# A float32 hybrid encoder layer: both heads' near-score products ahead of both minima, the second norm's reciprocal straight from PSUM, and three differences behind a split

## The chip, the cores and the metric

One core of a Trainium2 chip runs the whole layer as one program. The metric is the device time of one execution in microseconds (us). The layer has one batch element, 1024 positions, a model width of 1024 and float32 inputs and outputs. A difference of about 0.2% (2.6 us) is what the measurement of this kernel can tell from none.

## The reference, cut to what matters

```python
u = rms_norm(h, mix_norm_gain);  proj = u @ w_in
aq, ak, av, dqkv, dgate, da, db = split(proj)
# A: band attention, 8 heads of 64, chunks of 64, own chunk + 8 past ones
scores = einsum(q, k_band) * 64**-0.5 + rel_bias ;  p = softmax(where(valid, scores, min)) ; o = p @ v_band
# B: gated DeltaNet, 4 heads of 128: conv + SiLU, L2 norms, chunked delta rule over a state S, gated norm
h = h + concat[rms_norm(A), B] @ w_out
z = rms_norm(h, ffn_norm_gain) @ w_ff1          # norm over the width, per position: x * rsqrt(mean(x*x) + EPS)
h = h + square(relu(z)) @ w_ff2
```

## The kernel before, in words

**Stages.** The program first projects the input (0 to about 355 us of the profiled execution), then runs attention and the delta rule interleaved (to about 597 us), then the output projection `out_proj` (to about 684 us), the first feed-forward product `ff1` (to about 990 us) and the second, `ff2`. A float32 operand of the large products is split into a high and a low part (`split`, line 201: a cast on ScalarE, line 202, and a difference on VectorE or GpSimd, line 203), and three TensorE matmuls stand for one.

**Who sets the order.** Tile's scheduler orders each engine's instructions, with one exception: inside `attention` the TensorE order is the order in which the code is written (`manual_schedule`). A planner in that function, with a `Clock` of assumed costs, picks at each step the next piece: `score`, `flip`, `multiply`, `finish`, `turn`, or a step of the delta rule (`delta_state` S, `delta_out` O, `delta_merge` M, `delta_fin` F). Each engine runs its queue in order.

**A unit of attention** is one group of four heads g, one tile of 128 queries t, and one pair of heads pp: 2 x 8 x 2 = 32 units. `score` makes, for each of the two heads e of the pair, the near scores (the last 256 keys) into one half of one PSUM tile `t_sb` (`product`, matmuls at line 914) and takes their minimum with the bias (VectorE, line 930; a second small instruction reads the accumulated minimum into `t_nm`). Then come the far scores `t_sa` of each head in a PSUM tile of its own, with a minimum at line 941 that starts from the near one. ScalarE takes the exponentials (lines 949 and 953). `flip` transposes them (`t_tpb` at line 970, `t_tpa` at 986) and copies the results out on VectorE or ScalarE (lines 976, 991), `multiply` makes the product with the values (`t_o`, 1009), and `finish` transposes and scales it (1031, 1033); for the second group, eight times in all, `finish` also makes a root mean square on ScalarE and GpSimd (`t_r`) and scales by it on VectorE (line 1040). Tile puts semaphores between instructions of two engines that touch the same PSUM tile in the same bank, whichever columns they touch.

**The second norm** is in `ff1`. `norm_col` (line 1277) sums the squares into eight columns `hcol` with one matmul each (line 1283), multiplies and adds EPS on VectorE (line 1285), and takes the reciprocal (line 1287) into `r_col`. `norm_row` spreads `r_col` over all partitions (`hrow`, line 1293), and ScalarE copies that to `r2` (line 1295). The result is the square of the norm's scale, since the hidden values are squared.

**The second feed-forward product** uses a scheme of seven products instead of eight for each block kb of four (`p1`, `p5`, `p2`, `p3`, `p6`, `p7`, `p4`). Each `product` calls a `prep` that makes sums and differences of quarters on VectorE, then splits both operands (the low parts are named `p50a_l`, `p50b_l` for product 5 of block 0), then multiplies (line 1425). The differences the change touches are those of line 1508 (`s1 - a11`, for product 3) and line 1517 (`a11 - a21`, for product 7), each once per half i, so four per block.

Of the kernel before, what the change touches and what calls it, by code (L numbers as in the profile page):

```python
# [8 lines left out]
F32 = mybir.dt.float32  # L9
F32R = mybir.dt.float32r  # L10
AF = mybir.ActivationFunctionType
ALU = mybir.AluOpType
AX = mybir.AxisListType

P = 128
SEQ = 1024
DM = 1024
NKT = DM // P
NT = SEQ // P
# [9 lines left out]
EPS = 1e-6  # L29
# [12 lines left out]
LATENCY, MARGIN = 250, 400  # L42
# [5 lines left out]
class Clock:  # L48
# [16 lines left out]
    def pe(self, cost):  # L65
        self.now += cost
        return self.now + LATENCY
# [32 lines left out]
def hymba_kernel(  # L100
# [63 lines left out]
    warm = bank(ps_o, "warm")  # L164
    for i in range(WARM):
        nc.tensor.matmul(warm[:, 0:P], ones, ones, start=True, stop=True)
    ident = cpool.tile([P, P], F32, name="ident")
    make_identity(nc, ident)
    tri_u = mpool.tile([P, P], F32, name="tri_u")
# [658 lines left out]
    def attention(after, delta, values, outputs):  # L828
# [89 lines left out]
        def score(g, t, pp):  # L918
            T = tiles[g, t]
            n, k0, kb, nm = (T[k] for k in ("n", "k0", "kb", "nm"))  # L920
            wa, wb = (kb - k0) * P, (t + 1 - kb) * P
            cost = 0
            done = T["done"][pp] = []
            bk = bank(ps_a, f"{n}_sb{pp}")
            sb = page("u" if g or t > 1 else "wr", f"{n}_pb{pp}")
            for e in range(2):
                i = 2 * pp + e
                c = slice(e * 256 + 256 - wb, e * 256 + 256)
                cost += product(g, T, i, bk, c.start, kb, t + 1)
                nc.vector.tensor_tensor_reduce(sb[:, c], bk[:, c], new[g][pp][:, c], -1.0, 3.0e38,  # L930
                                               ALU.add, ALU.min, nm[:, 4 + i:5 + i])
                done.append(on("v", 180 + wb * 1.25, pe(30 + wb * 0.9)))
            give("a", done[1])
            sa = [None, None]
            if wa:
                for e in range(2):
                    i = 2 * pp + e
                    bk = bank(ps_a, f"{n}_sa{i}")
                    cost += product(g, T, i, bk, 0, k0, kb)
                    sa[e] = page("u", f"{n}_pa{i}")  # L940
                    nc.vector.tensor_tensor_reduce(sa[e][:, 0:wa], bk[:, 0:wa], old[g][i][:, 384 - wa:384], -1.0,  # L941
                                                   nm[:, 4 + i:5 + i], ALU.add, ALU.min, nm[:, i:i + 1])
                    done[e] = on("v", 305 + wa * 1.04, pe(max(234, wa * 0.92)))
                    give("a", done[e])
            for e in range(2):
                i = 2 * pp + e
                c = slice(e * 256 + 256 - wb, e * 256 + 256)
                m = nm[:, i:i + 1] if wa else nm[:, 4 + i:5 + i]
                nc.scalar.activation(sb[:, c], sb[:, c], AF.Exp, bias=m, scale=-1.0,  # L949
                                     accum_out=T["sums"][:, 4 + i:5 + i])  # L950
                done[e] = on("s", 480 + wb * 0.85, done[e])
                if wa:
                    nc.scalar.activation(sa[e][:, 0:wa], sa[e][:, 0:wa], AF.Exp, bias=m, scale=-1.0,  # L953
                                         accum_out=T["sums"][:, i:i + 1])
                    done[e] = on("s", 480 + wa * 0.83, done[e])
            T["s"][pp] = sa, sb
# [282 lines left out]
    def ff1(R, started, psw, pools):  # L1239
# [37 lines left out]
        def norm_col():  # L1277

            acc = page2("ut4", "acc")
            nc.sync.dma_start(out=acc, in_=sq_dr)  # L1280
            ps = psw.tile([P, 1024], F32, tag="bk", name="hcol")
            for q in range(NT):
                nc.tensor.matmul(ps[:, q:q + 1], acc[:, q * P:(q + 1) * P], ones[:, 0:1], start=True, stop=True)
            with tc.issue_after(held[-1][2]):
                m = nc.vector.tensor_scalar(r_col, ps[:, 0:NT], 1.0 / DM, EPS, ALU.mult, ALU.add)
                with tc.issue_after(m.ins), tc.high_priority():
                    nc.vector.reciprocal(r_col, r_col)

        def norm_row():

            ps = psw.tile([P, 1024], F32, tag="bk", name="hrow")
            for q in range(NT):
                nc.tensor.matmul(ps[:, q * P:(q + 1) * P], r_col[:, q:q + 1].broadcast_to([P, P]), ident,
                                 start=True, stop=True)
            nc.scalar.copy(r2.rearrange("p a t -> p (a t)"), ps)

        def block(sb):
            def lw(tag, name, kh, c):
# [102 lines left out]
    def ff2(psw, pools):  # L1401
# [7 lines left out]

        y = {i: [wide(t, 0), wide(t, 1)] for i, t in y.items()}  # L1410
        y[7] = [page2("y7", f"y7_{i}") for i in range(2)]
        side = [0]

        def load_h(t, j, hf, m):
            nc.sync.dma_start(out=two(t), in_=h_dr[j, hf, :, 2 * m:2 * m + 2, :])
# [1 line left out]
        def product(name, prep, by_rows=False):  # L1417
            t = "AB"[side[0]]
            side[0] ^= 1
            ps = [psw.tile([P, 1024], F32, tag="bk", name=f"{name}{m}") for m in range(4 if by_rows else 2)]  # L1420
            def step(i, k, q):
                (ah, al), (bh, bl) = ops[i]
                s = slice(k * 512 + q * P, k * 512 + (q + 1) * P)
                for m, (l, r) in enumerate(((ah, bh), (ah, bl), (al, bh))):
                    nc.tensor.matmul(part(ps[q], 0) if by_rows else part(ps[q // 2], q % 2), l[:, s], part(r, k),  # L1425
                                     start=(i + k + m == 0), stop=(i + k + m == 4))

            ops = []
            for i in range(2):
                ab = []  # L1430
                for o, src in zip("ab", prep(i)):
                    hi = page2("h" + t, f"{name}{o}{i}_h", F32R)
                    lo = page2("l" + t, f"{name}{o}{i}_l", F32R)
                    split(src, hi, lo, nc.scalar, nc.vector)
                    ab.append((hi, lo))
                ops.append(ab)
                if not by_rows:
                    for k in range(2):
                        for q in range(4):
                            step(i, k, q)  # L1440
            if by_rows:
                for q in range(4):
                    for i in range(2):
                        for k in range(2):
                            step(i, k, q)
            return ps
# [7 lines left out]
        for kb in range(nb):  # L1454
# [50 lines left out]
                return s1[i], b11[i]  # L1505

            def prep3(i):
                tt(s1[i], s1[i], a11[i], ALU.subtract)
                tt(a12[i], a12[i], s1[i], ALU.subtract)
                return a12[i], b22[i]  # L1510

# [2 lines left out]
                return s1[i], b11[i]  # L1514

            def prep7(i):
                tt(a21[i], a11[i], a21[i], ALU.subtract)
                tt(b12[i], b22[i], b12[i], ALU.subtract)
                return a21[i], b12[i]

# [3 lines left out]

            accumulate(1, product(f"p1{kb}", lambda i: (a11[i], b11[i])))
            accumulate(5, product(f"p5{kb}", prep5))
            accumulate(2, product(f"p2{kb}", lambda i: (a12[i], b21[i])))
            if last:
                merge(nc.gpsimd, 2, 1)
# [124 lines left out]
```

## Time and profile before

| what | value |
| --- | --- |
| time, median of 3 runs | 1321.31 us (1320.35 to 1322.62) |
| the profiled execution's own time | 1308.9 us |
| its span, first to last instruction | 1307.1 us |
| TensorE busy / weight loads busy | 1249.8 us (96%) / 1038.5 us (79%) |
| VectorE, ScalarE, GpSimd busy | 933.2, 548.1, 289.9 us |
| mean granted TensorE clock | 0.993 |

The profiled execution is 12.4 us shorter than the median of the timed runs; 1.8 us of its time lie outside the span. The profile's names: PE is TensorE's matmul, PEld its weight load, DVE VectorE, ACT ScalarE, POOL GpSimd. `L914` is line 914 of the kernel before; `t_sb<-ks,t_q` is output and inputs by the program's names. A row of waits gives the total, the number and the longest of the waits of one engine at one line for one releaser.

### The profile page before, as it was taken

The page shows a single profiled execution, that of the slowest core. Times are in us where ns is not written, and L with a number is a line of the kernel's source. Part 1 is how long each engine was busy: PE and PEld are TensorE (multiplying, and loading weights), DVE is VectorE, ACT ScalarE, POOL GpSimd, SP SyncE. Part 2 cuts the span into 40 slices and gives each one's busy share as a digit, 9 for nine tenths or more (in the row PEclk, how much of TensorE's full clock was granted, in tenths as well). Part 3 has the DMA queues.
Part 4 walks back from the last instruction along what each step waited for, and adds up shares of the span by engine and source line. Part 5 has one row for each costly group of instructions (what it writes and reads, how often), then busy time and mean ns, then how long its engine had stood idle before and what let it go on. Part 6 is the DMA issues. An engine that isn't in the chain of part 4 may idle for free.

```text
span 1307.1 us, 18026 instructions
## 1 busy us (share of the span) xinstructions
PE 1249.8 (96%) x6684; PEld 1038.5 (79%) x6684; DVE 933.2 (71%) x1389; ACT 548.1 (42%) x899; POOL 289.9 (22%) x486
## 2 busy tenths in 40 slices
PE   9999999999988888789999999999999999999998
PEld 7778878788777777677778788888887888888886
DVE  7899978655045556664528877766668988897988
ACT  8232222232254545562527444444464443333331
POOL 5425451444023333364220000000000000000034
PEclk9999999999999999899999999999999999999999
DMA  6214354566574423113423343233257733423002
GB/s 220 70 44 142 94 150 127 101 177 161 182 220 112 128 73 88 33 58 115 143 88 130 129 140 102 94 100 126 99 193 272 261 112 98 144 66 111 17 33 96
DMA packets 135400, 158.53 MB, mean 121 GB/s; under 512 B 31761, under 2 KB 79377, under 8 KB 134801
## 3 DMA queue, kind: packets, MB, share of 16 engines
q1 hardware_dynamic: 117216, 135.11, 33.7%
q10 hardware_dynamic: 18096, 22.29, 5.0%
q8 instruction: 52, 0.85, 0.3%
q14 instruction: 36, 0.29, 0.1%
HBM read 109.91 MB, written 47.45 MB: 120 GB/s over the span
## 4 chain that ended last, share of the span: by engine, by line
PE 57%; DVE 8%; ACT 2%; issue 2%; POOL 2%; DMA 1%; POOLq 1%; SPq 0%; DVEq 0%; ACTq 0%
PE q L1329 21%; PE p L1425 20%; PE op L221 5%; PE t_o L1009 2%; PE t_sb L914 1%; PE t_sa L914 1%; PE t_tpb L970 1%; PE c_pv L515 1%; DVE t_pb L930 1%; PE t_tpa L986 1%; PE c_pq L515 1%; POOLq L1649 1%; PE c_pS L515 0%; POOL wo_l L203 0%; DVE y L1497 0%
## 5 line engine op out<-in xcount | busy, mean ns | idle before, releaser
L1497 POOL TENSOR_TENSOR y<-y,y 128x1024 f32<-128x1024 f32 x6 | 19.3, 3242 | 590.5 <-DVE y L1493 571.7
L930 DVE CUSTOM_DVE_ANT_0 t_pb<-t_sb,biasn 128x256 f32<-128x256 f32 (+1 forms) x64 | 25.8, 404 | 53.6 <-PE t_sb L914 53.5
L1493 DVE TENSOR_TENSOR y<-y,p 128x1024 f32<-128x1024 f32 x46 | 55.1, 1214 | 5.4 <-PE p L1425 4.5
L914 PE MATMUL t_sb<-ks,t_q 128*128 128x256 f32 (+1 forms) x144 | 32.6, 320 | 23.8 <-DVE t_nm L930 23.2
L221 PE MATMUL op<-mh,wo_h 128*128 128x512 f32 x128 | 50.9, 398 | 3.5 <-ACT wo_h L202 3.2
L221 PE MATMUL op<-mh,wo_l 128*128 128x512 f32 x128 | 48.8, 392 | 1.9 <-POOL wo_l L203 1.9
L949 ACT ACTIVATE t_pb<-t_pb,t_nm 128x256 f32<-128x256 f32 (+1 forms) x64 | 31.4, 490 | 45.4 <-DVE t_nm L941 40.5
L221 PE MATMUL op<-ml,wo_h 128*128 128x512 f32 x128 | 50.1, 392 | 0.0
L914 PEld LDWEIGHTS t_sb<-ks,t_q 128*128 128x128 f32 x144 | 21.5, 195 | 30.3 <-DVE t_nm L930 29.9
L221 PEld LDWEIGHTS op<-mh,wo_h 128*128 128x128 f32 x128 | 24.1, 188 | 10.2 <-ACT wo_h L202 4.5
L1215 POOL TENSOR_TENSOR op_q<-op_q 128x512 f32<-128x512 f32 x14 | 19.1, 1364 | 56.4 <-ACT op_q L1214 56.3
L1208 DVE TENSOR_TENSOR h<-op,op_x 128x512 f32<-128x512 f32 x16 | 10.9, 686 | 28.3 <-PE op L221 28.3
L221 PEld LDWEIGHTS op<-mh,wo_l 128*128 128x128 f32 x128 | 24.0, 188 | 8.1 <-POOL wo_l L203 2.9
L986 PE MATMUL t_tpa<-ident,t_pa 128*128 128x128 f32 x120 | 21.9, 295 | 8.4 <-ACT t_ta L991 3.5
L941 DVE CUSTOM_DVE_ANT_0 t_pa<-t_sa,biaso,t_nm 128x384 f32<-128x384 f32 (+2 forms) x48 | 24.6, 548 | 5.2 <-PE t_o L1009 4.8
L221 PEld LDWEIGHTS op<-ml,wo_h 128*128 128x128 f32 x128 | 24.1, 188 | 4.8
L221 PE MATMUL g_ps<-uh,wg_h 128*128 128x512 f32 x64 | 25.4, 396 | 1.3 <-ACT wg_h L202 1.3
L953 ACT ACTIVATE t_pa<-t_pa,t_nm 128x384 f32<-128x384 f32 (+2 forms) x48 | 26.3, 549 | 0.0
L221 PE MATMUL g_ps<-uh,wg_l 128*128 128x512 f32 x64 | 25.2, 393 | 0.4 <-POOL wg_l L203 0.4
L221 PE MATMUL dq_ps<-uh,wdq_h 128*128 128x512 f32 x64 | 25.5, 398 | 0.0
L221 PE MATMUL dv_ps<-uh,wdv_l 128*128 128x512 f32 x64 | 25.4, 398 | 0.0
L221 PE MATMUL aq_ps<-waq_h,uh 128*128 128x512 f32 x64 | 25.4, 399 | 0.0
(1107 smaller groups left out, 4322.5 us busy)
## 6 DMA issues: line engine op xcount, KB each, us to landing
wa<-in_w_ff_dram SPq DMA_DIRECT2D x32, 512.0 KB
a<-in_w_ff_dram SPq DMA_DIRECT2D x32, 512.0 KB
b<-f_dr SPq DMA_DIRECT2D x32, 512.0 KB
f_dr<-yy ACTq DMA_DIRECT2D x16, 512.0 KB
t_q<-q_dr SPq DMA_DIRECT2D x30, 256.0 KB
f_dr<-zz ACTq DMA_DIRECT2D x13, 512.0 KB
ks<-k_dr SPq DMA_DIRECT2D x16, 256.0 KB
wo_r<-in_w_out_dram SPq DMA_DIRECT2D x16, 256.0 KB
```

The costliest lines, as they stand in the source:

```text
L221: nc.tensor.matmul(ps, a, b, start=(first and i == 0), stop=(last and i == n - 1))
L515: nc.tensor.matmul(ps[:, hs], lhs(h, hs), rhs(h, hs), start=True, stop=True)
L914: nc.tensor.matmul(o, q[m][:, i * P:(i + 1) * P], k[:, c], start=(m == 0), stop=(m == 1))
L930: nc.vector.tensor_tensor_reduce(sb[:, c], bk[:, c], new[g][pp][:, c], -1.0, 3.0e38, ALU.add, ALU.min, nm[:, 4 + i:5 + i])
L941: nc.vector.tensor_tensor_reduce(sa[e][:, 0:wa], bk[:, 0:wa], old[g][i][:, 384 - wa:384], -1.0, nm[:, 4 + i:5 + i], ALU.add, ALU.min, nm[: ...
L949: nc.scalar.activation(sb[:, c], sb[:, c], AF.Exp, bias=m, scale=-1.0, accum_out=T["sums"][:, 4 + i:5 + i])
L953: nc.scalar.activation(sa[e][:, 0:wa], sa[e][:, 0:wa], AF.Exp, bias=m, scale=-1.0, accum_out=T["sums"][:, i:i + 1])
L986: nc.tensor.transpose(tp[:, js], sa[e][:, js], ident)
L1009: nc.tensor.matmul(po[64 * e:64 * e + 64, pp * P:(pp + 1) * P], vt[k0 + j][:, 64 * h:64 * h + 64], (ta[e] if j < na else tb)[:, c:c + P], ...
L1329: nc.tensor.matmul(part(ps, q), l[:, s], r, start=(k + m == 0), stop=(k == 3 and m == 2))
L1425: nc.tensor.matmul(part(ps[q], 0) if by_rows else part(ps[q // 2], q % 2), l[:, s], part(r, k), start=(i + k + m == 0), stop=(i + k + m == 4))
L1493: nc.vector.tensor_tensor(y[i][m], y[i][m], ps[m], op)
```

## The change

1. `score` multiplies the near scores of both heads, and only then takes both minima, in the same order of heads. The planner books both products' TensorE time first, and both minima from the then current time; the sum of costs that it books is the same. (`cost`, which the old line added up, isn't used elsewhere.)
2. `norm_col` adds the EPS inside PSUM by one more matmul of ones with a small constant tile `epsc` (128 x 8, set once at the start by GpSimd), so that the line with the multiplication and addition on VectorE is gone; the reciprocal reads PSUM directly and stands behind the same instruction as the removed line, with high priority. The factor `DM` moves into the ScalarE copy of `norm_row`.
3. In `ff2`, the second of the two low parts of product 5's last split, `early`, is what the differences of `prep3` (`s1 - a11`) and `prep7` (`a11 - a21`) are now issued behind on VectorE, in every block. Three of the four differences of a block stood ahead of that low part before (both of product 7, one of product 3) and so move.

```diff
+    epsc = cpool.tile([P, NT], F32, name="epsc")
+    nc.gpsimd.memset(epsc, EPS * DM / P)
...
             for e in range(2):
                 i = 2 * pp + e
                 c = slice(e * 256 + 256 - wb, e * 256 + 256)
-                cost += product(g, T, i, bk, c.start, kb, t + 1)
+                product(g, T, i, bk, c.start, kb, t + 1)
+                pe(30 + wb * 0.9)
+            for e in range(2):
+                i = 2 * pp + e
+                c = slice(e * 256 + 256 - wb, e * 256 + 256)
                 nc.vector.tensor_tensor_reduce(sb[:, c], bk[:, c], new[g][pp][:, c], -1.0, 3.0e38,
                                                ALU.add, ALU.min, nm[:, 4 + i:5 + i])
-                done.append(on("v", 180 + wb * 1.25, pe(30 + wb * 0.9)))
+                done.append(on("v", 180 + wb * 1.25, clock.now + LATENCY))
...
+            nc.tensor.matmul(ps[:, 0:NT], ones, epsc, start=True, stop=False)
             for q in range(NT):
-                nc.tensor.matmul(ps[:, q:q + 1], acc[:, q * P:(q + 1) * P], ones[:, 0:1], start=True, stop=True)
-            with tc.issue_after(held[-1][2]):
-                m = nc.vector.tensor_scalar(r_col, ps[:, 0:NT], 1.0 / DM, EPS, ALU.mult, ALU.add)
-                with tc.issue_after(m.ins), tc.high_priority():
-                    nc.vector.reciprocal(r_col, r_col)
+                nc.tensor.matmul(ps[:, q:q + 1], acc[:, q * P:(q + 1) * P], ones[:, 0:1], start=False, stop=q == NT - 1)
+            with tc.issue_after(held[-1][2]), tc.high_priority():
+                nc.vector.reciprocal(r_col, ps[:, 0:NT])
...
-            nc.scalar.copy(r2.rearrange("p a t -> p (a t)"), ps)
+            nc.scalar.mul(r2.rearrange("p a t -> p (a t)"), ps, float(DM))
...
-                    split(src, hi, lo, nc.scalar, nc.vector)
+                    splits.append(split(src, hi, lo, nc.scalar, nc.vector)[1])
...
             def prep3(i):
-                tt(s1[i], s1[i], a11[i], ALU.subtract)
+                with tc.issue_after(early):
+                    tt(s1[i], s1[i], a11[i], ALU.subtract)
...
             def prep7(i):
-                tt(a21[i], a11[i], a21[i], ALU.subtract)
+                with tc.issue_after(early):
+                    tt(a21[i], a11[i], a21[i], ALU.subtract)
...
             accumulate(5, product(f"p5{kb}", prep5))
+            early = splits[-1]
```

What the first part does on TensorE, at unit (g=0, t=5, pp=0) as one of 32: the numbers in the names are the group and tile (`t05`) and the pair (`sb0`) or head (`sa0`, `ks011`); a row with `x2` is two equal instructions, and `DVE_49` is a wait on VectorE. Before:

```order
L914 MATMUL t05_sb0_4232<-ks010_3761,t05_q_4227 128x256 [waits DMAHW5_49,DMAHW4_49,DVE_49]
L914 MATMUL t05_sb0_4232<-ks010_3761,t05_q_4227 128x256
L914 MATMUL t05_sb0_4232<-ks011_3763,t05_q_4227 128x256 [waits DVE_49]
L914 MATMUL t05_sb0_4232<-ks011_3763,t05_q_4227 128x256
L914 MATMUL t05_sa0_4240<-ks000_3563,t05_q_4227 128x384 x2
L914 MATMUL t05_sa1_4245<-ks001_3565,t05_q_4227 128x384 x2
```

The same place after the change (the line is now 916):

```order
L916 MATMUL t05_sb0_4318<-ks010_3758,t05_q_4313 128x256 [waits DMAHW6_49,DMAHW5_49]
L916 MATMUL t05_sb0_4318<-ks010_3758,t05_q_4313 128x256
L916 MATMUL t05_sb0_4318<-ks011_3760,t05_q_4313 128x256 x2
L916 MATMUL t05_sa0_4326<-ks000_3565,t05_q_4313 128x384 x2
L916 MATMUL t05_sa1_4331<-ks001_3567,t05_q_4313 128x384 x2
```

The matmuls stand in the same order, and the second head's no longer wait for VectorE. Around the units the planner's choices come out otherwise: from the first score to the last piece of attention the delta-rule pieces, flips and products stand at other places between the scores, and the scheduler orders VectorE, ScalarE, GpSimd and the load queue anew there.

The second norm on VectorE, in `ff1`: `hcol` is the PSUM tile with the sums, `q6_0a_l`, `q3_0a_l` and `q7_0a_l` are low parts of weights for products of block 0, `t3l0` one of an activation, and `h01`, `h10` are differences of hidden quarters. Before, from the last low part ahead of the removed line:

```order
L203 TENSOR_TENSOR q6_0a_l_7595<-ws1_0_7550,q6_0a_h_7594 128x1024
L1270 TENSOR_TENSOR h01_7185<-h11_7056,h01_7185 128x1024 x2
L1285 TENSOR_SCALAR r_col_152<-hcol_7535 128x8
L203 TENSOR_TENSOR q3_0a_l_7651<-wa12_0_7383,q3_0a_h_7650 128x1024
L1270 TENSOR_TENSOR h10_6899<-h00_6655,h10_6899 128x1024 x2
L203 TENSOR_TENSOR t3l0_7700<-h01_7185,t3h0_7699 128x1024
L1287 RECIPROCAL r_col_152<-r_col_152 128x8
```

And after:

```order
L205 TENSOR_TENSOR q6_0a_l_7597<-ws1_0_7552,q6_0a_h_7596 128x1024
L1276 TENSOR_TENSOR h01_7187<-h11_7058,h01_7187 128x1024 x2
L1292 RECIPROCAL r_col_154<-hcol_7537 128x8
L205 TENSOR_TENSOR q3_0a_l_7653<-wa12_0_7385,q3_0a_h_7652 128x1024
L1276 TENSOR_TENSOR h10_6901<-h00_6684,h10_6901 128x1024 x2
```

The reciprocal stands where the removed line stood, four long instructions earlier.

The differences on VectorE, in `ff2`, block 0: `s10`, `s11` are the two halves of s1, `a210`, `a211` those of a21, `b110`, `b111` those of b11, `yy7` the last hidden tile of `ff1`. Before, from the second sum of product 5:

```order
L1503 TENSOR_TENSOR s11_0_9606<-a211_0_9473,a221_0_9477 128x1024
L1517 TENSOR_TENSOR a210_0_9471<-a110_0_9463,a210_0_9471 128x1024
L203 TENSOR_TENSOR p50a0_l_9575<-s10_0_9571,p50a0_h_9574 128x1024
L1504 TENSOR_TENSOR b110_0_9467<-b120_0_9479,b110_0_9467 128x1024
L1517 TENSOR_TENSOR a211_0_9473<-a111_0_9465,a211_0_9473 128x1024
L1504 TENSOR_TENSOR b111_0_9469<-b121_0_9481,b111_0_9469 128x1024
L1337 TENSOR_TENSOR yy7_9179<-yy7_9179,r2_7380 128x1024
L1508 TENSOR_TENSOR s10_0_9571<-s10_0_9571,a110_0_9463 128x1024
L203 TENSOR_TENSOR p50b0_l_9579<-b110_0_9467,p50b0_h_9578 128x1024
```

And after:

```order
L1508 TENSOR_TENSOR s11_0_9608<-a211_0_9475,a221_0_9479 128x1024
L205 TENSOR_TENSOR p50a0_l_9577<-s10_0_9573,p50a0_h_9576 128x1024
L1509 TENSOR_TENSOR b110_0_9469<-b120_0_9481,b110_0_9469 128x1024
L1509 TENSOR_TENSOR b111_0_9471<-b121_0_9483,b111_0_9471 128x1024
L1342 TENSOR_TENSOR yy7_9181<-yy7_9181,r2_7382 128x1024
L205 TENSOR_TENSOR p50b0_l_9581<-b110_0_9469,p50b0_h_9580 128x1024
L205 TENSOR_TENSOR p50a1_l_9612<-s11_0_9608,p50a1_h_9611 128x1024
L205 TENSOR_TENSOR p50b1_l_9616<-b111_0_9471,p50b1_h_9615 128x1024
L1514 TENSOR_TENSOR s10_0_9573<-s10_0_9573,a110_0_9465 128x1024
L1524 TENSOR_TENSOR a210_0_9473<-a110_0_9465,a210_0_9473 128x1024
L1524 TENSOR_TENSOR a211_0_9475<-a111_0_9467,a211_0_9475 128x1024
```

The three differences that stood ahead of the low part `p50b0_l` now stand behind all four low parts of product 5. TensorE's order changes there too: two matmuls of product 2 that stood among those of product 5 move behind them, and in products 3 and 6 groups of matmuls change places.

2 lines of the change are left out of this document (1 added, 1 removed).

## The prediction

> **What bounds the kernel now.** I read the page first, then the busy times of the attention stage, the waits, the timeline of single units, and the chain that ended last. The page:
>
> ```profile
> span 1307.1 us, 18026 instructions
> PE 1249.8 (96%) x6684; PEld 1038.5 (79%) x6684; DVE 933.2 (71%) x1389; ACT 548.1 (42%) x899; POOL 289.9 (22%) x486
> ```
>
> TensorE is busy all but 57 us of the span. The busy times of the attention stage, 355 to 597 us (PE, PEld, DVE, ACT, POOL, each with its count, then granted clock and DMA):
>
> ```profile
> 355.00:597.00 242.00, 201.19 (x1850) 176.91 (x1850) 141.73 (x433) 130.12 (x383) 93.76 (x235) 0.96 0.37 107
> ```
>
> 242.0 - 201.2 = 40.8 us of TensorE's idle time lie here, and no other engine is near full. The waits for the whole span say what it is (total, number, longest), and name the two other waits that the change touches:
>
> ```profile
> PE t_sb L914 <- DVE t_nm L930: 23.2, 31, 1.5
> PE t_tpa L986 <- ACT t_ta L991: 3.5, 1, 3.5
> ...
> PE p L1425 <- DVE p50b_l L203: 1.8, 1, 1.8
> ...
> PE hrow L1293 <- DVE r_col L1287: 1.7, 1, 1.7
> ```
>
> One wait is more than half of the stage's idle time: the near product of a pair's second head waits in 31 of 32 units until VectorE has taken the first head's minimum. The other waits share 40.8 - 23.2 = 17.6 us. One unit in the timeline (start, duration, idle before and releaser):
>
> ```profile
> 383.94 0.64 PE L914 MATMUL t_sb<-ks,t_q 128*128 128x128 f32 x4
> 384.62 0.42 DVE L930 CUSTOM_DVE_ANT_0 t_pb<-t_sb,biasn 128x256 f32<-128x256 f32 x1
> 384.97 0.08 DVE L930 DVE_READ_ACCUMULATOR2_ANT t_nm<- 128x1 f32 x1
> 385.11 0.66 PE L914 MATMUL t_sb<-ks,t_q 128*128 128x128 f32 x4 [0.53 <-DVE t_nm L930]
> 385.61 0.91 PE L914 MATMUL t_sa<-ks,t_q 128*128 128x384 f32 x4
> 385.81 0.42 DVE L930 CUSTOM_DVE_ANT_0 t_pb<-t_sb,biasn 128x256 f32<-128x256 f32 x1 [0.76 <-PE t_sb L914]
> ```
>
> VectorE was free at once here, so 0.53 us is the bare round trip. The chain that ended last passes through it: the page gives its shares of the span by engine and by line.
>
> ```profile
> PE 57%; DVE 8%; ACT 2%; issue 2%; POOL 2%; DMA 1%; POOLq 1%; SPq 0%; DVEq 0%; ACTq 0%
> PE q L1329 21%; PE p L1425 20%; PE op L221 5%; PE t_o L1009 2%; PE t_sb L914 1%; PE t_sa L914 1%; PE t_tpb L970 1%; PE c_pv L515 1%; DVE t_pb L930 1%; PE t_tpa L986 1%; PE c_pq L515 1%; POOLq L1649 1%; PE c_pS L515 0%; POOL wo_l L203 0%; DVE y L1497 0%
> ```
>
> The near minimum (`t_pb`, line 930) stands among its largest pieces that are not TensorE's.
>
> **The change, part by part.** *Near scores.* The second product no longer waits. From start to start it takes 385.61 - 385.11 = 0.50 us, but the second began 385.11 - 383.94 = 1.17 us after the first; without the wait that is 0.50, so 0.67 us go where the row shows 0.53 idle. The other 0.14 is the first product's pipeline running dry. So 31 x 0.14 = 4.3 us come on top of the 23.2: TensorE could save 27.5 us.
>
> The weight loads' own wait at this place bounds that from above:
>
> ```profile
> PEld t_sb L914 <- DVE t_nm L930: 29.9, 32, 1.7
> ```
>
> The Trainium skill ("Perfetto Trace Analysis", Identifying the Most-Contended Engine) holds matmul busy time to be a poor measure because matmuls are pipelined, and the weight loads' busy time the better one. This trace agrees in direction, with 29.9 against 23.2; a sum by the weight loads would come out 2.4 us better than mine.
>
> Not all of 27.5 stays saved. In 31 waits, 31 x 0.53 = 16.4 us are bare round trip; the other 23.2 - 16.4 = 6.8 us are VectorE being late with something else, and TensorE will meet that lateness at its next wait. I take them off whole: 20.7. And with TensorE earlier, the copies on VectorE and ScalarE for which the other waits stand have less time. Those waits (17.6 us now) can stay as they are, or at worst double. I take a quarter more, 4.4 us, nearer to no growth because VectorE has 100 and ScalarE 112 us free in the 242. That leaves 16.3 us. The minimum of the first head now starts after the second product, 0.50 us later; queued behind it on VectorE are the second near minimum, both far ones, and whatever the scheduler put next, and ScalarE's exponentials wait for them. What that is worth is the first rival.
>
> Since the planner's times shift, the order of everything else in the stage is drawn anew. The clock is one more thing that this can touch. Four stretches of the stage ran at half clock, each shown here behind the stretch before it:
>
> ```profile
> 394.00:397.40 3.40, 2.58 (x22) 2.17 (x23) 2.36 (x10) 0.72 (x3) 1.70 (x7) 0.99 0.08 12
> 397.40:400.80 3.40, 3.40 (x18) 3.40 (x18) 0.00 (x0) 3.09 (x9) 1.58 (x3) 0.51 0.87 205
> 428.00:431.40 3.40, 2.67 (x66) 2.39 (x65) 0.91 (x2) 1.44 (x4) 2.18 (x4) 1.00 0.45 151
> 431.40:434.90 3.50, 3.50 (x25) 3.44 (x22) 1.08 (x4) 1.09 (x3) 0.74 (x2) 0.51 0.02 5
> 523.60:527.00 3.40, 0.59 (x5) 0.58 (x5) 1.91 (x9) 3.30 (x11) 0.00 (x0) 1.00 0.00 0
> 527.00:533.80 6.80, 5.58 (x25) 5.28 (x24) 3.97 (x12) 3.98 (x12) 4.74 (x15) 0.50 0.26 72
> 561.20:564.50 3.30, 1.50 (x12) 1.03 (x11) 2.87 (x11) 2.62 (x10) 1.13 (x6) 1.00 0.03 5
> 564.50:568.00 3.50, 2.97 (x14) 2.68 (x14) 0.64 (x3) 1.54 (x4) 2.53 (x8) 0.51 0.28 75
> ```
>
> In the half-clock stretches 3.40 + 3.50 + 5.58 + 2.97 = 15.45 us of TensorE's time were busy, so they cost up to 7.7 us. They follow stretches busy for 76, 79, 17 and 45%. Only the first holds a wait of the removed kind as its main gap, so I take no change, with 7.7 us either way as bounds.
>
> The Trainium skill ("TensorE: Matmul & The Clock Gate", Part 1) has the clock halved only behind a whole idle window of about 3.4 us. By that rule waits of half a microsecond have no hand in it and the sum stays as it is. The trace differs: two of four halvings follow windows in which TensorE worked three quarters of the time, so I keep the other case as a rival.
>
> *Second norm.* The rows of its sums, its two VectorE steps and the spread:
>
> ```profile
> L1283 PE MATMUL hcol<-ones,acc x16: 163/251/251, 706.6 to 708.2; 128*128 128x1 f32 x16
> ...
> 716.22 0.16 DVE L1285 TENSOR_SCALAR r_col<-hcol 128x8 f32<-128x8 f32 x1
> ...
> 720.83 0.20 DVE L1287 RECIPROCAL r_col<-r_col 128x8 f32<-128x8 f32 x1
> ...
> 721.17 2.02 PE L1293 MATMUL hrow<-ident,r_col 128*128 128x128 f32 x16 [1.66 <-DVE r_col L1287]
> ```
>
> The reciprocal moves from 720.83 to where the removed step was, 716.22. TensorE came to `hrow` at 721.17 - 1.66 = 719.51, so the wait goes whole: 1.7 us. What could be late next are `t3l` and `q7`'s low part on VectorE, due only after product 3, 24 matmuls on. Against it stands one more matmul of 8 columns: 16 rows for eight column sums within 1.6 us make 0.1 us a row, so two rows are 0.2 us. ScalarE multiplies instead of copying, in one instruction as before: nothing, at most 0.1 us either way. The constant `epsc` is one small GpSimd fill at the start; a like one, 128 x 16, took 111 ns there, and TensorE's first matmul waits for `ones`, which is filled ahead of it: nothing.
>
> *Three differences.* The place in the timeline, and the piece of the chain behind it:
>
> ```profile
> 999.12 1.22 DVE L1517 TENSOR_TENSOR a<-a,a 128x1024 f32<-128x1024 f32 x1
> ...
> 1002.53 1.22 DVE L1517 TENSOR_TENSOR a<-a,a 128x1024 f32<-128x1024 f32 x1
> ...
> 1005.93 1.22 DVE L1508 TENSOR_TENSOR s<-s,a 128x1024 f32<-128x1024 f32 x1
> 1005.94 0.61 PE L1425 MATMUL p<-p50b_h,p50a_h 128*128 128x512 f32 x2
> ...
> 1007.07 1.22 DVE L203 TENSOR_TENSOR p50b_l<-b,p50b_h 128x1024 fp32r<-128x1024 f32 x1
> ...
> 1008.34 260.98 PE p L1425 x1150
> ```
>
> VectorE is full here, at 1.14 us from one instruction to the next (1005.93 to 1007.07). With three of them gone from ahead of it, `p50b_l` is done at about 1007.07 + 1.22 - 3.42 = 1004.9, ahead of TensorE at 1005.94: the 1.8 us go. The moved four end by about 1011.8, and product 2 is due only after 48 matmuls of 0.227 us (260.98 / 1150), at 1016.8, so its four splits still come in time. If they did not, half of the 1.8 would come back. In the later blocks no wait shows here that could go.
>
> *Sum.* 16.3 + 1.7 - 0.2 + 1.8 = 19.6 us of the profiled execution's 1308.9 (span 1307.1, 1.8 around it), which makes 1289.3. The timed runs' median is 12.4 us longer for reasons that this trace doesn't show; I take the same microseconds off it: 1321.3 - 19.6 = 1301.7 us.
>
> **The rivals.** *The minima pace the stage.* If the softmax chain and not TensorE's queue sets the pace, what counts is when a pair's second minimum starts. Before: 385.81, that is 1.87 us after the first product. After: the second product starts at 384.44, the minima can start 0.70 us behind it (385.81 - 385.11), at 385.14, and the second follows 0.35 us later (384.62 to 384.97), at 385.49. That is 0.32 us a unit, 10.2 us in 32, and with 3.3 from the other parts 13.5: 1307.8 us. For it speaks that ScalarE waits for minima more than for anything else; against it that neither engine is near full.
>
> *The clock stays up.* With a denser TensorE queue the four half-clock stretches disappear: another 7.7 us, 1294.0 us.
>
> *Nothing is won in attention.* All that TensorE saves returns at the transposes and copies, since the delta rule's steps and the copies set the pace: only the 3.3 us of the feed-forward parts, 1318.0 us. Against it: those waits are 17.6 us now, and would have to grow to 40.
>
> *Slower: VectorE holds its queue for GpSimd.* The new order may put the scaling of line 1040, which waits for a GpSimd chain, ahead of a unit's minima more often. It happened once among the eight such steps:
>
> ```profile
> 522.30 0.49 DVE L1040 TENSOR_SCALAR t_on<-t_on,t_r 128x512 f32<-128x512 f32 x1 [2.54 <-POOL t_r L198]
> ...
> 526.41 0.55 PE L986 MATMUL t_tpa<-ident,t_pa 128*128 128x128 f32 x3 [3.50 <-ACT t_ta L991]
> ```
>
> It cost TensorE 3.40 - 0.59 = 2.8 us idle and half of the 5.58 at half clock, 5.6 together. Four more would eat the gain (22.4); five make 28.0 - 19.6 = 8.4 us slower, 1329.7 us. In the new order VectorE has about as much other work between these steps and what they wait for as before, which speaks against it.
>
> **How the numbers follow.** The forecast has 0.50, minima 0.17, clock 0.15, nothing won 0.10, slower 0.08. What the measurement can tell is 0.2%, 2.6 us, or 1318.7 and below; nothing won lies on that edge and is halved. Faster: 0.50 + 0.17 + 0.15 + 0.05 = 0.87; same 0.05; slower 0.08. The forecast's own bounds are the other waits unchanged (4.4 better) or doubled (13.2 worse): 1297 to 1315. Low end: the clock's 1294.0 and the 6.8 us kept after all, 1287; high end 1314, which leaves the last two cases out.
>
> **What would show it.** Right: no wait of `t_sb` on `t_nm` (at most some 7 us of VectorE's lateness at other places), TensorE idle between 355 us and the stage's end at 18 to 27 us, no wait at `hrow` and at `p50b_l`. Wrong: the waits of `t_tpb`, `t_tpa` and `t_o` on copies grown by over 13 us, or more half-clock stretches than four with rows of line 1046 (the old 1040) waiting for GpSimd ahead of them.

## The result and the profile after

| | before | after |
| --- | --- | --- |
| time, median (lowest to highest, 4 runs each) | 1320.83 us (1318.72 to 1322.62) | 1301.27 us (1300.20 to 1302.42) |
| ratio, with its 95% interval | | 0.9853 (0.9835 to 0.9871) |
| the profiled execution: time, span, mean granted clock | 1308.9, 1307.1 us, 0.993 | 1302.0, 1300.1 us, 0.984 |

The change takes off 19.6 us, as forecast; that the tenth agrees is luck, as the parts show. The two profiled executions differ by 6.9 us only, so the total alone says little about the steps. The head of the page of after:

```profile
span 1300.1 us, 18013 instructions
PE 1252.7 (96%) x6686; PEld 1043.8 (80%) x6686; DVE 931.8 (72%) x1389; ACT 546.5 (42%) x898; POOL 289.9 (22%) x487
```

I cut both programs at the same instructions: the first near score, the first matmul of `ff1`, the first of `ff2`. Rows of the windows: stretch, its length, busy time of PE, PEld, DVE, ACT, POOL, granted clock, DMA share. Before:

```profile
355.50:684.80 329.30, 285.75 (x2215) 245.13 (x2213) 175.38 (x471) 161.08 (x432) 119.93 (x262) 0.97 0.36 107
684.80:990.10 305.30, 303.64 (x1355) 251.78 (x1356) 222.35 (x193) 152.20 (x150) 1.29 (x1) 1.00 0.37 123
990.10:1307.10 317.00, 310.06 (x1367) 256.16 (x1365) 280.06 (x236) 119.84 (x121) 26.03 (x8) 1.00 0.36 123
```

After:

```profile
355.30:671.70 316.40, 284.91 (x2215) 248.28 (x2213) 173.39 (x472) 160.19 (x431) 119.44 (x262) 0.95 0.38 112
671.70:977.10 305.40, 304.24 (x1357) 251.92 (x1358) 222.00 (x192) 151.84 (x150) 1.29 (x1) 1.00 0.36 123
977.10:1300.10 323.00, 313.02 (x1367) 258.08 (x1365) 280.40 (x236) 119.87 (x121) 26.04 (x8) 0.99 0.35 121
```

Attention with the output projection is 12.9 us shorter. `ff1`, with the new norm, has the length that it had. `ff2`, with the moved differences, is 6.0 us longer. TensorE's waits of after (total, number, longest) name what is new:

```profile
PE t_sb L916 <- DMA t_q<-q_dr: 7.0, 1, 7.0
PE t_tpa L992 <- ACT t_tb L982: 6.1, 5, 3.1
PE p L1430 <- DVE p30b_l L205: 4.7, 1, 4.7
PE t_tpa L992 <- DVE t_ta L997: 3.5, 1, 3.5
...
PE q L1334 <- ACT q_1a_h L204: 0.9, 1, 0.9
```

The 23.2 us on `t_nm`, the 1.7 at `hrow` and the 1.8 at `p50b_l` are gone, all as forecast. New are a near score that waits 7.0 us for its queries, a wait of 4.7 us at product 3's low part, and 0.9 us at a weight of `ff1`. A unit with eight near matmuls of 128 x 128, as in the one shown of before, in the timeline of after:

```profile
393.36 1.09 PE L916 MATMUL t_sb<-ks,t_q 128*128 128x128 f32 x8
394.28 0.92 PE L916 MATMUL t_sa<-ks,t_q 128*128 128x384 f32 x4
394.87 0.41 DVE L936 CUSTOM_DVE_ANT_0 t_pb<-t_sb,biasn 128x256 f32<-128x256 f32 x1
395.20 0.08 DVE L936 DVE_READ_ACCUMULATOR2_ANT t_nm<- 128x1 f32 x1
395.20 0.42 DVE L936 CUSTOM_DVE_ANT_0 t_pb<-t_sb,biasn 128x256 f32<-128x256 f32 x1
```

From the first near matmul to the first far one it takes 394.28 - 393.36 = 0.92 us, where before took 385.61 - 383.94 = 1.67. That is 0.75 less, of which 0.53 was shown as idle: in this pair of units the pipeline's part is 0.22 us, where the forecast had 0.14.

**The clock.** Timed runs of one kernel differ mostly in how long TensorE was held at half clock. Of 37 timed executions of before that stand beside the experiments, the shortest and the longest:

| span | mean granted clock | span x clock |
| --- | --- | --- |
| 1309.3 us | 0.991 | 1297.5 us |
| 1323.0 us | 0.978 | 1293.9 us |
| all 37: median 1318.4 us | median 0.983 | mean 1296.3 us, standard deviation 1.5 |

Span times clock takes most of that out: the spans have a standard deviation of 3.1 us and lie within 13.7 us, the values of span times clock 1.5 and 6.1. It takes off somewhat too much, since it falls where the span is long (1293.9 against 1297.5 in the table), so what is put down to the clock below is rather too large. For after (4 runs) the median span is 1299.4 us at 0.986, the mean of span times clock 1281.2. Of the 19.0 us between the median spans, 1296.3 - 1281.2 = 15.1 us are work and waits by this measure, and 3.9 us the clock. The profile that the forecast was worked from, with 0.993, shows before at its best: it lost 1307.1 x 0.007 = 9 us to the clock, where the median execution lost 22.

### The profile page after: what moved, and what is told of

It is laid out like the page before. It is cut to its first block, busy times and chain, and to the rows that moved or that the text cites. A ratio compares the mean times of both kernels' runs of the same rounds, so it can differ in the third digit from the quotient of the medians.

```text
span 1300.1 us, 18013 instructions
## 1 busy us (share of the span) xinstructions
PE 1252.7 (96%) x6686; PEld 1043.8 (80%) x6686; DVE 931.8 (72%) x1389; ACT 546.5 (42%) x898; POOL 289.9 (22%) x487
## 4 chain that ended last, share of the span: by engine, by line
PE 47%; DVE 8%; DMA 3%; ACT 2%; issue 2%; POOL 1%; POOLq 1%; SPq 0%; DVEq 0%; ACTq 0%
PE q L1334 19%; PE p L1430 19%; PE op L223 6%; DMA b<-f_dr 1%; DMA y<-h_dr 1%; PE t_o L1015 1%; DVE h L1276 1%; POOLq L1657 1%; DVE y L1502 0%; DMA h_dr<-h 0%; DVE q_0a_l L205 0%; DMA a<-in_w_ff_dram 0%; PE t_sa L916 0%; DVE y L1498 0%; ACT t_pb L955 0%
## 5 line engine op out<-in xcount | busy, mean ns | idle before, releaser
L955 ACT ACTIVATE t_pb<-t_pb,t_nm 128x256 f32<-128x256 f32 (+1 forms) x64 | 31.3, 489 | 37.8 <-DVE t_nm L947 34.4
L916 PE MATMUL t_sb<-ks,t_q 128*128 128x256 f32 (+1 forms) x144 | 25.6, 310 | 7.0 <-DMA t_q<-q_dr 7.0
```

The costliest lines, as they stand in the source:

```text
L916: nc.tensor.matmul(o, q[m][:, i * P:(i + 1) * P], k[:, c], start=(m == 0), stop=(m == 1))
```

## The experiments

Times are medians; each run stands beside runs of before on the same chip, whose median is 1319.5 us beside the kernel before once more, part 1 alone, the old picks and part 3 alone, 1320.2 beside the new picks alone and half of the waits, and 1320.6 beside the other four.

**The kernel before, once more**, without an edit.

> The kernel before, unchanged, for a second profile. Its timed median (1320.8 us) is 11.9 us above its profiled execution (1308.9), while the kernel after shows 1302.0 profiled and 1301.3 timed. Theory A (the clock): the timed executions of before hold half-clock stretches that the first profile lacks; then this one comes out near 1320 with a mean granted clock near 0.975 instead of 0.993 and some 24 us more of half-clock stretches, and the near waits (t_sb on t_nm, 23.2 us in 31) unchanged. Rival (something outside the instructions): a profile as the first, 1309 us and clock 0.993.

Measured: 1316.0 us in one run, which is the profiled one. Clock, near waits and the stretch from the first near score to `ff1`:

```profile
core 0: 1314.2 us, clock 0.988
```

```profile
PE t_sb L914 <- DVE t_nm L930: 23.3, 32, 1.5
```

```profile
358.10:691.90 333.80, 290.15 (x2215) 248.68 (x2213) 174.93 (x471) 161.14 (x432) 120.09 (x262) 0.96 0.35 106
```

Theory A holds in kind, with less than it expected (1320 us and a clock of 0.975): the near waits are the same to a tenth, the clock is lower. From the first near score to `ff1` TensorE was idle 333.80 - 290.15 = 43.7 us, as in the first profile (43.6), but busy 290.2 us for the same 2215 matmuls, where it was 285.8. The forecast's waits can be trusted; its view of the clock couldn't.

**Part 1 alone.** The diff is the first hunk of the change, in `score`.

> Part 1 alone: near products of both heads first, second norm and differences as before. Theory A (the removed near waits are the gain, and part 3 takes some of it back): after's 19.6 us, less 1.7 for the norm, plus 6.3 which part 3 costs (4.7 of wait at p30b_l and 3.4 by the half clock behind it, less the 1.8 won at p50b_l): 24.2 us off, 1296.6 us; the 7 us wait of t_sb for the load of t_q near 372 us and the half clock behind it stay. Rival B (the attention stage gains only the 13.1 us that the two profiles show between the first score and ff1): 1307.7 us.

Measured: 1297.1 us (1294.3 to 1298.7), ratio 0.9841 (0.9815 to 0.9867): 22.5 us off.

```profile
356.30:673.00 316.70, 283.05 (x2214) 246.65 (x2213) 174.15 (x472) 159.84 (x431) 118.27 (x261) 0.95 0.37 111
```

```profile
PE t_sb L914 <- DMA t_q<-q_dr: 7.7, 1, 7.7
PE t_tpa L990 <- ACT t_tb L980: 6.1, 5, 3.2
```

Theory A holds, B doesn't. Part 1 alone takes off more than the whole change (22.5 against 19.6 us, though the two intervals of the ratio overlap), and it brings the wait for `t_q` with it.

**Products first, with the planner's old picks.** The bookings stay with the minima, so TensorE has the order of before in attention:

```diff
-                cost += product(g, T, i, bk, c.start, kb, t + 1)
+                product(g, T, i, bk, c.start, kb, t + 1)
+            for e in range(2):
+                i = 2 * pp + e
+                c = slice(e * 256 + 256 - wb, e * 256 + 256)
                 nc.vector.tensor_tensor_reduce(...)
                 done.append(on("v", 180 + wb * 1.25, pe(30 + wb * 0.9)))
```

> Products first as in part 1, but the planner books the old costs in the old order, so its picks and the TensorE order stay those of before; the second norm and the differences as before. Theory A (removing the waits is what wins, the picks don't matter): no t_sb wait on t_nm, 31 x (0.14 pipeline + 0.53 round trip) = 20.7 us off, 1300 us, and without a long wait for t_q it beats part 1 alone by no more than what that wait costs (7 idle, some 6 by the clock). Rival C (the new picks are what wins, and with the old ones the saved waits return at the transposes): the waits of t_tpa and t_tpb grow by over 13 us, the gain is under 8 us, 1313 us or more.

Measured: 1292.6 us (1289.1 to 1294.5), ratio 0.9806 (0.9777 to 0.9835).

```profile
357.10:665.20 308.10, 280.63 (x2215) 244.61 (x2213) 170.32 (x471) 160.42 (x432) 122.03 (x262) 0.96 0.38 115
665.20:971.70 306.50, 303.94 (x1354) 251.63 (x1355) 221.91 (x193) 151.99 (x150) 1.29 (x1) 1.00 0.36 122
```

```profile
PE t_sb L914 <- DMA t_q<-q_dr: 4.9, 1, 4.9
PE t_tpb L973 <- DVE mixa L1053: 3.3, 2, 2.7
PE t_tpa L989 <- ACT t_tb L979: 2.8, 3, 1.1
```

C falls: the waits at the transposes don't take the gain's place, and 27.0 us come off. That is 6.3 more than A had; by span times clock it is 1296.3 - 1276.0 = 20.3, and the rest is clock. The old picks are 4.5 us better than the new ones.

**The new picks alone**, with the old order of instructions:

```diff
-                done.append(on("v", 180 + wb * 1.25, pe(30 + wb * 0.9)))
+                pe(30 + wb * 0.9)
+            for e in range(2):
+                done.append(on("v", 180 + wb * 1.25, clock.now + LATENCY))
```

> Only the planner's bookings of part 1: its new picks, with the instructions in the old order (product, minimum, product, minimum), so TensorE has the order of part 1 alone and keeps the near waits. With the old and new picks, with and without the waits, this is the fourth of four. Theory A (the waits are the gain, and the new picks cost some 4.5 us, 1297.1 against 1292.6): 1320 + 4.5 = 1324.5 us, near waits of some 23 us in the profile, and a wait for t_q near 372 us. Rival C (the new picks win by themselves): 1312 us or less.

Measured: 1329.1 us (1325.2 to 1332.0), ratio 1.0065 (1.0041 to 1.0090): 8.8 us slower.

```profile
PE t_sb L914 <- DVE t_nm L930: 26.0, 32, 2.4
PE t_sb L914 <- DMA t_q<-q_dr: 5.1, 1, 5.1
```

With this the square is full (median time, and in brackets the mean of span times clock; the left column was timed on one chip, the right on another, and before's own medians there are 1320.2 and 1319.5 us):

| | near waits | no near waits |
| --- | --- | --- |
| old picks | 1320.2 us (1296.3) | 1292.6 us (1276.0) |
| new picks | 1329.1 us (1301.7) | 1297.1 us (1278.7) |

Removing the waits is worth 27.6 and 32.0 us, or 27.0 and 31.3 with the chips' 0.7 us taken off; by span times clock 20.3 and 23.0 of it are not clock. The new picks cost 8.8 and 4.5 us. So the gain is the waits', and the order that is drawn anew is a loss under both.

**Half of the waits.** As with the old picks, but products first only where g is 0: 16 of the 32 units.

> Products first with the old picks as before, but in the first group of heads only, 16 of the 32 units; the second group waits as before. Theory A (each removed wait is worth what it shows and the terms add up): about half of the 27.4 us that all 32 units gave, 13.5 us, so 1306.5 us, and 16 near waits with some 11.5 us left. Rival H (the first removed waits only shift time to the others, and the gain comes when all are gone): under 8 us, 1312 us or more.

Measured: 1306.7 us (1303.8 to 1310.0), ratio 0.9899 (0.9876 to 0.9922).

```profile
PE t_sb L914 <- DVE t_nm L934: 13.2, 16, 2.4
PE t_sb L914 <- DMA t_q<-q_dr: 6.6, 2, 5.7
```

Half of the waits, half of the gain in time (13.5 us), so H's bound of 8 us falls. Without the clock it is less than half: 1296.3 - 1289.0 = 7.3 us of 20.3. The rows say why: 10.0 us of near waits go and, at 0.22 us in 16 units, 3.5 of pipeline, but 6.6 us of waiting for `t_q` are new already here, and with all the near waits gone it is no longer than 4.9. So the terms add up only with that new wait counted, and H was right about this one wait.

**Part 3 alone.** The diff is the hunks in `ff2`.

> Part 3 alone: the differences of products 3 and 7 behind product 5's last low part. The forecast's step: 1.8 us off, 1319.0 us. Theory D (the scheduler, in block 0, puts the sums and low parts of product 6 ahead of the low parts of product 3, and TensorE stands 4.7 us at p30b_l, then half a clock for some 6.8 us): 6.3 us slower, 1327 us, with the same wait at p30b_l as after shows.

Measured: 1323.5 us (1315.1 to 1326.8), ratio 1.0036 (1.0015 to 1.0057): 4.0 us slower. Its `ff2`, from the first matmul on, and the only wait in it:

```profile
1003.20:1325.00 321.80, 311.80 (x1367) 257.11 (x1366) 280.63 (x236) 119.97 (x121) 26.04 (x8) 0.99 0.35 121
```

```profile
PE p L1425 <- DVE p30b_l L203: 4.7, 1, 4.7
```

The forecast's step is wrong in sign, D's mechanism is there, and the cost is less than D's 6.3 us: the half clock behind the wait lasted 3.4 us, where D had 6.8. VectorE in the timeline of after shows how the wait comes about:

```profile
1015.74 1.22 DVE L205 TENSOR_TENSOR p60a_l<-s,p60a_h 128x1024 fp32r<-128x1024 f32 x1
1016.88 1.22 DVE L205 TENSOR_TENSOR p60b_l<-b,p60b_h 128x1024 fp32r<-128x1024 f32 x1
1018.01 1.22 DVE L205 TENSOR_TENSOR p30a_l<-a,p30a_h 128x1024 fp32r<-128x1024 f32 x1
1019.15 1.22 DVE L205 TENSOR_TENSOR p30b_l<-b,p30b_h 128x1024 fp32r<-128x1024 f32 x1
```

Two low parts of product 6 stand ahead of those of product 3, which TensorE multiplies first. In before all four low parts of product 3 stand ahead of product 6's.

**The change, with product 3's low parts first.** In short form, for block 0, with `third` for the last low part of product 3:

```diff
+                    with tc.issue_after(third):
                         splits.append(split(src, hi, lo, nc.scalar, nc.vector)[1])
...
+                with tc.issue_after(third):
                     tt(b12[i], b22[i], b12[i], ALU.subtract)
...
+                with tc.issue_after(third):
                     tt(b21[i], b11[i], b21[i], ALU.subtract)
```

> The kernel after, but in block 0 of the second feed-forward product the low parts of product 6 and the differences for products 7 and 4 stand behind the last low part of product 3 on VectorE. Theory D (part 3 costs time because product 3's low parts come behind those of product 6): no wait at p30b_l, no half-clock stretch near 1020 us, the second product's length back from 323.0 to 315.3 us (317.1 of before less the 1.8 at p50b_l), so 7.7 us off after's 1301.3: 1293.6 us. Rival G (VectorE is simply short of time there, and the wait moves to product 6 or 7): the same length within 2 us, 1300 us.

Measured: 1294.0 us (1290.6 to 1296.1), ratio to before 0.9801 (0.9770 to 0.9832).

```profile
978.90:1294.20 315.30, 310.12 (x1367) 256.19 (x1365) 280.29 (x236) 119.81 (x121) 26.04 (x8) 1.00 0.36 124
```

The length is the expected one, 7.7 us under after's, and TensorE has no wait left in it. D is shown and G falls: VectorE had the time, only the order was wrong. The forecast's 1.8 us for part 3 are there (317.0 - 315.3 = 1.7) once product 3's low parts come first (the first hunk stands in product 6, the others in `prep7` and `prep4`).

**Part 2 alone.** The diff is the hunks in `norm_col` and `norm_row`, and `epsc`.

> Part 2 alone. One look, since 1.5 us are too few for a timing: what counts is the length of the first feed-forward product, from its first matmul to the first of the second product, 305.3 us in both profiles of before. The forecast's step: the 1.7 us wait at hrow goes, the added matmuls cost 0.2, so 303.8 us. Rival E (what is saved at hrow returns some 25 us later, at the low and the high part of a weight, q_1a, which ScalarE and VectorE deliver no earlier): 305.3 us, with waits of 0.2 and 0.9 us at q_1a as the profile of after shows them. The whole run can come out anywhere between 1308 and 1324 with the granted clock.

Measured: 1319.6 us. The first feed-forward product, and the wait in it:

```profile
695.50:1000.80 305.30, 304.28 (x1357) 251.96 (x1358) 221.91 (x192) 151.92 (x150) 1.29 (x1) 1.00 0.36 123
```

```profile
PE q L1330 <- ACT q_1a_h L204: 0.9, 1, 0.9
```

The length is unchanged to a tenth: E holds, with the wait at `q_1a_h`. The wait at `hrow` is gone; 0.9 us come back there, and TensorE's busy time is 304.28 - 303.64 = 0.6 us longer, where I had 0.2. The same 0.9 at `q_1a_h` stands in the run with the old picks, which has no part 2, and not in part 1 alone. It goes with the order of TensorE in `ff1`: part 1, part 3 and the new picks alone keep the order that `ff1` has in before, and have no such wait; all the other changed kernels have another order there, and the wait. With the old picks, where the wait comes without part 2, `ff1` is 306.5 us long, and 305.3 in the last run below, which has part 2: there the wait at `hrow` is a gain of 1.2 us. So the redrawn order seems to have taken the gain of part 2; that it makes the wait by itself wasn't tried.

**The change, with later loads held back.** The loads of values 4 to 7 and of the second group's keys now come behind the load of tile 3's queries:

```diff
+        def load_last():
+            with tc.issue_after(tiles[0, 3]["load"]):
                 load_values(range(4, NT))
                 load_keys(1, 0)
                 load_keys(1, 1)
```

> The kernel after, but the loads of the later values and of the second group's keys (12 loads of 256 KB) are held behind the load of tile 3's queries. Theory A (the 7.0 us wait of t_sb for t_q is queueing behind these loads, and the long half-clock stretch from 367 to 384 us follows from that idle time): the wait shrinks to under 3 us, the stretch to 7 us or less, together 4 to 5 us idle and some 4 us by the clock, 8 to 9 us off after's 1301.3: 1293 us. Rival F (the wait is for the buffer of the queries, which comes free only when tile 0's second score has run, and not for the other loads): the load still lands some 7 us behind its issue, 1301 us.

Measured: 1299.2 us (1297.0 to 1301.1), ratio to before 0.9842 (0.9811 to 0.9872): 2.0 us under after, less than the 2.6 that can be told from none, and not the 8 of A. In after, TensorE and the DMA engines around the wait (the windows' columns):

```profile
355.30:364.80 9.50, 9.33 (x54) 7.31 (x52) 2.62 (x16) 3.77 (x14) 2.53 (x12) 1.00 1.01 346
364.80:371.70 6.90, 0.01 (x1) 0.05 (x1) 0.55 (x3) 1.49 (x7) 0.00 (x0) 0.68 1.06 330
371.70:384.30 12.60, 12.60 (x74) 11.40 (x76) 5.43 (x28) 6.16 (x23) 1.10 (x3) 0.50 0.51 139
```

The DMA engines are full, and behind the empty stretch TensorE runs at half clock for 12.6 us. The load's issue and its first matmul in after:

```profile
364.53 2.51 SPq L897 DMA_DIRECT2D t_q<-q_dr  x4
...
371.69 1.19 PE L916 MATMUL t_sb<-ks,t_q 128*128 128x256 f32 x4 [6.97 <-DMA t_q<-q_dr]
```

With the loads held, SP's queue and the wait:

```profile
366.24 1.84 SPq L900 DMA_DIRECT2D t_q<-q_dr  x3
```

```profile
PE t_sb L920 <- DMA t_q<-q_dr: 4.4, 1, 4.4
```

The load is issued at 366.24 and its first matmul starts at 372.35, 6.1 us later. In after it was 371.69 - 364.53 = 7.2. So the held loads are about 1 us of that, and another 1.5 us because the load is now issued sooner after the first near score; together they are the 2.6 us by which the wait shrinks. F has the larger part, as far as this run goes: the queries have two buffers, and the load is issued only when tile 0's last score is done. In the old picks that score runs earlier (load at 359.1 us, and no wait for it); the new ones put the last block of the value projection (av_ps, some 5.5 us) ahead of it. But there the next load, issued at 368.6, is used at 375.6, 7.0 us later, with 4.9 us of waiting. Why a load takes 6 to 7 us isn't settled: with the loads held, the DMA engines are full again from 368.2 us on (share 0.98 and then 1.02). A third buffer wasn't tried.

**All three parts, the old picks, both mends.**

> All three parts of the change with the old picks of the planner, and with both mends, the held loads and product 3's low parts first. If the terms add up: 1292.6 us of the old picks alone, less the 4.9 us wait for t_q and 2 by the clock, less 1.8 at p50b_l, less 0 to 1.5 for the norm: 1283 us. If the attention stage's other waits take the place of what is removed: 1290 us or more.

Measured: 1287.2 us (1285.4 to 1289.2), ratio 0.9752 (0.9723 to 0.9781): the fastest here, 14 us under after.

```profile
PE op L223 <- ACT wo_h L204: 3.1, 3, 1.6
PE t_sb L920 <- DMA t_q<-q_dr: 2.8, 3, 1.7
...
PE op L223 <- POOL wo_l L205: 1.9, 2, 1.2
```

Its first feed-forward product:

```profile
666.00:971.30 305.30, 304.23 (x1356) 251.89 (x1357) 221.91 (x192) 151.50 (x150) 1.29 (x1) 1.00 0.36 123
```

Beside the old picks alone it gains 5.4 us and not the 9.6 of the sum: 2.8 of the 4.9 us for `t_q` are still there, and TensorE waits 5.0 us for weights of the output projection (3.1 for high parts, 1.9 for low), where that run had 4.2. By span times clock the two runs are only 1276.0 - 1274.9 = 1.1 us apart, so much of the 5.4 us may be clock. What is left of the difference isn't settled.

## Why the prediction was right, point by point

The total was right, and so was the main mechanism, but errors in the sum cancelled: part 1 alone took off 22.5 us where the sum had 16.3, part 2 nothing where it had 1.5, and part 3 cost 4.0 where it had 1.8 saved. So the 19.6 is luck; the direction and the mechanism are not.

**The near waits go, and that is the gain: right.** The square shows it (27.6 and 32.0 us with them against without), and half of them give half in time. The rival by which nothing is won in attention is out. So is the one by which the minima pace the stage: it allows 10.2 us there, and the square gives 20.3 and 23.0 without the clock.

**Size of that step: 27.5 less 11.2 forecast, 12.1 + 7.6 found.** From the window rows, TensorE's idle time between the marks fell from 329.30 - 285.75 = 43.6 to 316.40 - 284.91 = 31.5 us, by 12.1. That is 23.2 less 11.1, and I had 6.8 + 4.4 = 11.2. But of the 11.1, 7.0 are one wait for `t_q` that I hadn't seen; the remaining waits grew by 4 us, where the lateness and the copies' growth together should have made the 11.2. The pipeline term was too small: TensorE's busy time counted at full clock fell from 278.1 to 270.5 us, by 7.6 where I had 4.3; 0.22 us in 32 units are 7.0. Full clock means less half of the busy time in half-clock stretches, 15.3 us of it between the marks before and 28.8 after. The weight loads' wait of 29.9 us, which the forecast took as a bound, was the better measure of what the near waits cost: 23.2 + 7.0 = 30.2. The condition that TensorE be idle 18 to 27 us in the stage was missed by some 2 us, and would have held without the 7.0 for `t_q`:

```profile
355.30:596.70 241.40, 212.19 (x1899) 189.46 (x1898) 146.44 (x440) 130.45 (x383) 94.31 (x245) 0.93 0.39 110
```

That is 241.40 - 212.19 = 29.2 us.

**"I take no change" for the clock: wrong.** The median execution of before lost 22 us to the clock, not the 9 of the one profile, and after lost 18. With the waits the half-clock time shrinks too: 3.9 us of the gain are clock, and 7 to 9 us where the waits alone go (27.6 against 20.3, 32.0 against 23.0). That the denser queue is the reason is the plain reading; it wasn't tried apart. The rival of the clock was half right, at the median, though the profile of after has a longer half-clock time than that of before. The Trainium skill ("TensorE: Matmul & The Clock Gate", Part 1) has the gate that halves TensorE's clock watch a free-running window, and calls the time at half clock variable from run to run. The traces agree: two profiles of before with the same waits spent 15.3 and 28.9 us of TensorE's work at half clock.

**Second norm, 1.7 - 0.2: wrong in effect.** The wait went as foreseen and `ff1` got no shorter, with part 2 alone or in the whole change; with the old picks it did, by 1.2 us. The step that failed was to ask only for `t3l` and `q7` as next to be late, on VectorE, with the rest of the order as it stood; what came late was a high part on ScalarE, for an order of TensorE that was drawn anew.

**Three differences, 1.8: wrong in sign.** The failing step was "its four splits still come in time": it was right for product 2 and stopped there. The new order of VectorE's queue, which was at hand, has product 6's low parts ahead of product 3's; I read it up to the moved instructions only.

**The slower rival** didn't come: VectorE waited for GpSimd's `t_r` at line 1046 for 2.1 us in two places, where it was 3.2 in two before. The redrawn order does cost 4.5 to 8.8 us, but at other places: with the near waits kept, these grow from 23.2 to 26.0 us and 5.1 for `t_q` come on top.

With the parts by themselves: 22.5 - 4.0 + 0 = 18.5, against 19.6 for the change.

## What to carry to other kernels

Where an edit shifts a planner's or a scheduler's times, price the edit and the order that is drawn anew apart: here the edit was worth 27 us, and the new order costs 4 to 9 us, which the old bookings would have kept. Follow a moved instruction to the end of the queue, not only to the next one due, since what stands ahead of what two products later decided the sign. And before a profile is used as the base of a sum, hold its granted clock against the clocks of the timed runs.

## What the runs showed of the hardware

TensorE went to half clock behind a stretch in which its instructions had covered nearly all the time. In the run with the held loads, around the column sums of the second norm:

```profile
695.40:698.80 3.40, 3.24 (x23) 2.68 (x22) 3.40 (x4) 3.40 (x4) 0.00 (x0) 0.99 0.00 0
698.80:702.20 3.40, 3.40 (x10) 2.64 (x9) 3.40 (x5) 2.94 (x4) 0.00 (x0) 0.51 0.53 154
```

3.24 of 3.40 us are busy, and the next 3.4 us run at 0.51. Sixteen of the 23 matmuls there are `hcol` sums with one column of output each. In the stretch that was 79% busy ahead of a halving in the first profile of before there were 66 small ones, most of them 32 x 32. That the gate which halves the clock counts work in the array and not time covered would fit both; no run here tests it.

The Trainium skill's rule (same page and section) has the clock halved after an idle window of about 3.4 us. In after it holds for the wait at `p30b_l`, with no matmul in the 3.4 us ahead of the halving; ahead of the one at `t_q` TensorE was still busy for 0.73 us of them:

```profile
363.90:367.30 3.40, 0.73 (x3) 0.28 (x2) 1.45 (x9) 2.39 (x11) 0.00 (x0) 0.99 1.05 401
367.30:384.40 17.10, 12.71 (x76) 11.55 (x78) 5.43 (x28) 6.26 (x23) 1.10 (x3) 0.50 0.64 177
...
1015.80:1019.20 3.40, 0.00 (x0) 0.00 (x0) 3.40 (x5) 2.44 (x3) 0.00 (x0) 1.00 0.02 3
1019.20:1026.00 6.80, 5.58 (x13) 4.47 (x14) 6.80 (x8) 0.00 (x0) 0.00 (x0) 0.50 0.92 303
```

It doesn't hold for the column sums. The forecast read the rule as the only cause of a halving, and these traces show others.

The wait of 7 us for `t_q` brought 17.1 us at half clock, which began within it (367.3 to 384.4). For the last 12.6 us of them TensorE was busy without a gap, and still at half clock, so the clock cost 6.3 us, about as much as the wait itself.
